# A decoder trunk on one core: another order at the ends of the feed forwards

## The chip, the cores and the metric

The kernel runs on one core of one Trainium2 chip. The metric is the device time of one execution in microseconds (us). The core's engines each work through their own list of instructions in order: PE multiplies matrices (PEld is its loading of weights), DVE and ACT work on tiles elementwise, POOL does a few additions, SP issues most of the transfers. An instruction waits until what it reads is written and what it overwrites has been read.

## The reference

Two layers, each a feed forward, a mixer and a second feed forward, on 512 tokens of 1024 channels in float32:

```
for l in range(2):
    x = x + 0.5 * swiglu(rms_norm(x, ffn1_norm[l]), gate1[l], up1[l], down1[l])
    u = rms_norm(x, mix_norm[l])
    ...                       # four branches on u (attention, convolution, sparse attention, retention)
    x = x + merged @ w_out[l]
    x = x + 0.5 * swiglu(rms_norm(x, ffn2_norm[l]), gate2[l], up2[l], down2[l])
swiglu(x) = (silu(x @ w_gate) * (x @ w_up)) @ w_down          # 1024 -> 2816 -> 1024
rms_norm(x, g) = x / sqrt(mean(x * x) + 1e-6) * g
```

## The kernel before, in words

Activations lie transposed: `XT[:, d]` holds channels 128 d to 128 d + 127 of all 512 tokens. Every float32 product is made as three products of rounded halves, hi x hi, hi x lo and lo x hi. So each weight block is split: ACT writes `whi` (L213), DVE subtracts and writes `wlo` (L214). Both lie in four rotating buffers, so the split of unit n waits until unit n - 4 has been multiplied.

A feed forward (`ffn`) goes through 11 pairs p of hidden tiles. The gate and up products of a pair are made by a seven-product scheme of Strassen's kind over 2 x 2 blocks: `comb_in` forms seven combinations of the input, the factors 0 to 6 (`Ahi`, `Alo` for 0 to 3, the tiles `E` for 4 to 6), for four groups c of two channel tiles each; DVE forms seven combinations of the weights (sums at L414). A product (`product`, L408) is 24 matmuls of 128 x 256, six for each group c. In program order a pair makes products 0 (bank `sc`), 1 (`pv`), 2 (`sc`), 3 (`tp`), 4 (`sc`), 5 (`tp`), 6 (`sc`). Between them ACT copies partial results out of the bank (`snap`, L389), and the next product that adds into the bank waits for that copy. At the end of a pair comes `h`, hi (L488, ACT) and lo (L489, DVE), which the down products read. They run in units between later pairs (`down_unit`, L525, matmuls of 128 x 512), and the last four pairs' (hidden tiles 14 to 21) in a tail of eight units, one for each output tile d. Each adds into `XT` on DVE (L527) and calls `done(d)`.

`done` starts what comes next on that tile: at the end of a first feed forward the mixer's norm (`norm_in`: hi, lo, a square on ACT, its sum into `acc` on POOL, L321), at the end of the first layer's second feed forward the same with `comb_in`, at the very end `flush(d)`: four transposes on PE (L1176), a copy on ACT (L1178), a store of 256 KB issued on ACT's queue (L1180). The w_out products in front of a second feed forward (L1161, add at L1162) call `norm_in` with `comb_in` too. `norm_end` sums `acc` over channels on PE (L327), takes the inverse root on DVE in twelve small rows, spreads it as a diagonal `z` (L335), multiplies it by ones (L339, ACT copies it out as `R`, L341). Its two results lie in bank `tp` (two buffers). The next feed forward calls it after its second product; only the end of the first pair (L482, L484) needs `R`.

`Line.go` prepares the weights of the unit three ahead of the one it runs, and the last units of one stretch prepare the first three of the next. A scheduler decides on each engine's list from this program order, priorities and its own estimate of times; a tile's buffers are given out in program order. `tc.issue_after(x)` holds all instructions traced in its block that are on x's engine behind x in that engine's list.

FFN1(l) and FFN2(l) are the feed forwards of layer l. FFN1(0) gets its factors from the input, FFN2(0) and FFN2(1) from w_out, FFN1(1) from the tail of FFN2(0).

Of the kernel before, what the change touches and what calls it, by code (L numbers as in the profile page):

```python
# [71 lines left out]
def body(tc, ins, out):  # L72
# [203 lines left out]
    def comb_in(d, gain, src=None):  # L276
# [10 lines left out]
        with tc.high_priority() if len(st["order"]) == 4 else ExitStack():  # L287
# [3 lines left out]
            dve.tensor_tensor(F[:, 4], F[:, 5], F[:, 7], op=OP.subtract)  # L291
            dve.scalar_tensor_tensor(F[:, 2], F[:, 4], -1.0, F[:, 0], op0=OP.mult, op1=OP.subtract)
            dve.tensor_tensor(lo[:, 0:2], F[:, 0:2], fv(hi[:, 0:2]), op=OP.subtract)  # L293
            dve.tensor_tensor(F[:, 3], F[:, 0], F[:, 7], op=OP.subtract)
            act.activation(hi[:, 2:4], F[:, 2:4], AF.Copy)
            dve.scalar_tensor_tensor(F[:, 6], F[:, 2], -1.0, F[:, 1], op0=OP.mult, op1=OP.subtract)
            dve.tensor_tensor(lo[:, 2:4], F[:, 2:4], fv(hi[:, 2:4]), op=OP.subtract)
            for u in range(3):
                act.activation(e[u][:, 0, c], F[:, 4 + u], AF.Copy)
                dve.tensor_tensor(e[u][:, 1, c], F[:, 4 + u], fv(e[u][:, 0, c]), op=OP.subtract)  # L300
# [11 lines left out]
    def norm_in(d, gain, comb=False):  # L312
        XT = ph["XT"]
        (comb_in if comb else split_in)(d, gain)
        if not ph["sq"]:
            ph["sq"] = True
            act.activation(st["acc"], XT[:, d], AF.Square)
        else:
            sq = ph["fp"].tile([128, T], F32, name="z", tag="z", bufs=2)
            act.activation(sq, XT[:, d], AF.Square)  # L320
            pool.tensor_tensor(st["acc"], st["acc"], sq, op=OP.add)  # L321

    def norm_end(ss=None):
        if ss is None:
            ss = tp_t()[:, :NT]
# [10 lines left out]
        ps = tp_t()  # L336
# [10 lines left out]
    class Line:  # L347
# [13 lines left out]
        def go(self, nxt=None):  # L361
            n = len(self.items)
            for i in range(n):
                self.prep(i + 1 + AHEAD)
# [5 lines left out]
    def ffn(wg, wu, wd, norm, done):  # L370
# [139 lines left out]
        def down_unit(f0, nf, d0, nd, l0, ln, end):  # L510

            def prep():
# [3 lines left out]
                return split(rawds[key][:, :, (d0 - l0) * 128:(d0 - l0 + nd) * 128], (nf, nd * 128), False)  # L516

            def run(w):
                whi, wlo = w
                for j in range(nd):  # L520
                    ps = mm_t()
                    for k in range(nf):
                        h, b = hs[(f0 + k) // 2], (f0 + k) % 2
                        for n, (x, s) in enumerate(((whi, 0), (whi, 1), (wlo, 0))):
                            pe.matmul(ps, x[:, k, j * 128:(j + 1) * 128], h[:, s, b], start=k == 0 and n == 0, stop=k == nf - 1 and n == 2)  # L525
                    XT = ph["XT"]
                    dve.scalar_tensor_tensor(XT[:, d0 + j], ps, 0.5, XT[:, d0 + j], op0=OP.mult, op1=OP.add)  # L527
                    if end:
                        done(d0 + j)

            return prep, run


# [719 lines left out]
```

## Time and profile before

| what | value |
|---|---|
| three runs | 2836.33, 2837.72, 2836.96 us, median 2836.96 |
| the profiled execution, its own time | 2836.33 us |
| its span, first to last instruction | 2834.6 us |
| busy: PE, DVE, ACT, POOL | 2782.0, 1941.5, 1266.1, 54.0 us |
[...]

The profile is of one execution. A PE row's time includes the pipeline's end, so rows overlap their successors: rates are read from start to start, idle time from the brackets behind a row.

### The profile page before, as it was taken

Reading aid. Unit: us, or ns where it says so; the run is one execution under the profiler, and the core shown is the slowest. Engines: PE = TensorE matmul, PEld = TensorE weight load, DVE = VectorE, ACT = ScalarE, POOL = GpSimd, SP = SyncE. Lnnn points to the kernel's source line nnn. Section 1 sums busy time; section 2 is a strip of 40 time slices with the busy share of each in tenths; the row PEclk is TensorE's granted clock in tenths of the full one; section 3 lists DMA queues with packets and bytes.
Section 4 is the critical chain, followed back from the end, with each engine's and each line's share of the span. In section 5 each row is a group of like instructions: output and inputs, shape, how many; then the busy total and the mean of one; then the engine's idle time right before and its main releaser. Section 6 shows DMA issues by size and latency. Waiting matters only on the chain.

```text
span 2834.6 us, 40078 instructions
## 1 busy us (share of the span) xinstructions
PE 2782.0 (98%) x16295; PEld 2352.9 (83%) x16295; DVE 1941.5 (68%) x3329; ACT 1266.1 (45%) x2012; POOL 54.0 (2%) x39
## 2 busy tenths in 40 slices
PE   6999999999999999999999999999999999999998
PEld 6999978788776688999889998777887657799996
DVE  7787755547567478786887866564565765888782
ACT  6444443433356355444544444343323663554441
POOL 0000010000000010000000001000000000100000
PEclk8999999999999999999999999999999999999999
DMA  4323332132420252323323233312324203423312
GB/s 140 115 86 109 117 101 89 42 121 60 149 90 1 66 172 75 111 91 97 120 75 118 83 97 116 103 60 75 117 71 137 60 1 89 159 95 101 112 57 74
DMA packets 238461, 265.94 MB, mean 94 GB/s; under 512 B 7292, under 2 KB 210884, under 8 KB 238276
## 3 DMA queue, kind: packets, MB, share of 16 engines
q1 hardware_dynamic: 233876, 261.20, 28.7%
q8 instruction: 128, 2.10, 0.3%
q10 hardware_dynamic: 4400, 2.17, 0.3%
q14 instruction: 57, 0.47, 0.1%
HBM read 257.06 MB, written 6.29 MB: 93 GB/s over the span
## 4 chain that ended last, share of the span: by engine, by line
PE 82%; DVE 2%; ACT 2%; issue 0%; DMA 0%; POOL 0%; ACTq 0%; DVEq 0%; POOLq 0%
PE mm L231 20%; PE sc L408 13%; PE mm L525 13%; PE mm L701 6%; PE tp L408 6%; PE mm L637 5%; PE mm L1161 3%; PE pv L969 3%; PE pv L408 3%; PE tp L959 2%; PE pv L637 2%; PE sc L921 1%; PE sc L922 1%; ACT whi L213 1%; PE tp L909 0%; DVE wlo L214 0%
## 5 line engine op out<-in xcount | busy, mean ns | idle before, releaser
L213 ACT ACTIVATE whi<-raw 128x1024 fp32r<-128x1024 f32 (+2 forms) x368 | 352.3, 958 | 757.0 <-PE mm L231 282.1
L214 DVE TENSOR_TENSOR wlo<-raw,whi 128x1024 fp32r<-128x1024 f32 (+2 forms) x368 | 402.8, 1098 | 185.1 <-ACT whi L213 178.8
L525 PE MATMUL mm<-h,whi 128*128 128x512 f32 x1408 | 445.4, 397 | 3.4 <-ACT h L488 2.7
L231 PE MATMUL mm<-Ahi,whi 128*128 128x512 f32 x864 | 342.2, 396 | 0.0
L231 PE MATMUL mm<-Ahi,wlo 128*128 128x512 f32 x864 | 340.6, 394 | 0.0
L231 PE MATMUL mm<-Alo,whi 128*128 128x512 f32 x864 | 340.3, 394 | 0.0
L525 PEld LDWEIGHTS mm<-h,whi 128*128 128x128 f32 x1408 | 260.9, 188 | 64.5 <-ACT h L488 3.5
L213 ACT ACTIVATE whi<-s 128x1024 fp32r<-128x1024 f32 x176 | 186.5, 1060 | 260.6 <-PE sc L408 71.7
L525 PE MATMUL mm<-h,wlo 128*128 128x512 f32 x704 | 278.8, 396 | 0.0
L214 DVE TENSOR_TENSOR wlo<-s,whi 128x1024 fp32r<-128x1024 f32 x176 | 214.6, 1219 | 46.1 <-ACT whi L213 45.5
L408 PE MATMUL sc<-E,whi 128*128 128x256 f32 x1408 | 225.1, 282 | 9.0 <-ACT sn L389 7.4
L408 PEld LDWEIGHTS sc<-E,whi 128*128 128x128 f32 x1408 | 192.0, 190 | 10.6 <-ACT sn L389 8.8
L527 DVE SCALAR_TENSOR_TENSOR XT<-mm,XT 128x512 f32<-128x512 f32 x128 | 88.0, 688 | 155.4 <-PE mm L525 155.4
L231 PEld LDWEIGHTS mm<-Ahi,wlo 128*128 128x128 f32 x864 | 162.5, 188 | 34.8 <-issue 3.6
L231 PEld LDWEIGHTS mm<-Ahi,whi 128*128 128x128 f32 x864 | 162.4, 188 | 34.9 <-issue 2.0
L231 PEld LDWEIGHTS mm<-Alo,whi 128*128 128x128 f32 x864 | 162.7, 188 | 31.6 <-issue 1.6
L213 ACT ACTIVATE whi<-rawd 128x1024 fp32r<-128x1024 f32 (+1 forms) x96 | 94.7, 989 | 150.5 <-PE sc L408 69.8
L525 PEld LDWEIGHTS mm<-h,wlo 128*128 128x128 f32 x704 | 132.6, 188 | 32.1
L408 PE MATMUL sc<-Ahi,whi 128*128 128x256 f32 x704 | 144.2, 287 | 6.0 <-ACT whi L213 3.8
L408 PE MATMUL sc<-Alo,whi 128*128 128x256 f32 x704 | 143.1, 285 | 2.5 <-DVE Alo L293 2.5
L214 DVE TENSOR_TENSOR wlo<-rawd,whi 128x1024 fp32r<-128x1024 f32 (+1 forms) x96 | 110.3, 1149 | 50.6 <-ACT whi L213 50.3
L408 PE MATMUL sc<-Ahi,wlo 128*128 128x256 f32 x704 | 142.7, 284 | 0.5 <-DVE wlo L214 0.5
(299 smaller groups left out, 5617.1 us busy)
## 6 DMA issues: line engine op xcount, KB each, us to landing
raw<-in_w_in_dram SPq DMA_DIRECT2D x66, 1024.0 KB, 6.8
raw<-in_ffn_w_gate_dram SPq DMA_DIRECT2D x44, 1024.0 KB, 5.3
raw<-in_ffn_w_up_dram SPq DMA_DIRECT2D x44, 1024.0 KB, 7.8
rawd<-in_ffn_w_down_dram SPq DMA_DIRECT2D x32, 1024.0 KB, 5.1
rawd<-in_ffn_w_down_dram SPq DMA_DIRECT2D x16, 768.0 KB, 4.4
raw<-in_w_branch_dram SPq DMA_DIRECT2D x8, 1024.0 KB, 7.6
raw<-in_w_branch_dram SPq DMA_DIRECT2D x16, 512.0 KB, 8.9
raw<-in_w_out_dram SPq DMA_DIRECT2D x8, 1024.0 KB, 8.6
```

Source lines behind the costliest of these rows:

```text
L213: act.activation(hi, src, AF.Copy)
L214: dve.tensor_tensor(lo, src, fv(hi), op=OP.subtract)
L231: pe.matmul(ps, x, y, start=first and j == 0, stop=last and j == len(passes) - 1)
L408: pe.matmul(ps[:, g * 256:(g + 1) * 256], x[:, g * 4 + c], factor(u, s, c), start=first and n == 0, stop=last and n >= 22, skip_group_chec ...
L525: pe.matmul(ps, x[:, k, j * 128:(j + 1) * 128], h[:, s, b], start=k == 0 and n == 0, stop=k == nf - 1 and n == 2)
L527: dve.scalar_tensor_tensor(XT[:, d0 + j], ps, 0.5, XT[:, d0 + j], op0=OP.mult, op1=OP.add)
L637: pe.matmul(ps[i][:, :n], a, w, start=kk == 0 and j == 0, stop=kk == KT - 1 and j == 2)
L701: pe.matmul(ps, x[:, k], v[:, k], start=k == 0 and j == 0, stop=k == 3 and j == 2)
L921: pe.matmul(ps[:, :n], q, kT[0][:, g, s0:s0 + n], start=True, stop=False)
L959: pe.transpose(ps[:, r * 128:(r + 1) * 128], P[4 * g + r][:, j * 128:(j + 1) * 128], ident)
L969: pv_last[0] = pe.matmul(pv[g * 64:(g + 1) * 64], V(g, j), pts[g], start=first and j == 0, stop=last and j == nblk - 1)
L1161: pe.matmul(ps, x[:, k], v, start=k == 0 and j == 0, stop=k == KT - 1 and j == 2)
```

## The change

In `comb_in` two DVE rows change places, and `st["made"]` keeps the last factor row. The last of the seven additions into `acc` goes from POOL to DVE, in the `comb` case behind `made`. `norm_end` takes its two results' banks from `mm` (three buffers) where a feed forward calls it, still from `tp` at the end of a first feed forward. `Line.go` puts what the first four units of a feed forward prepare (units 3 to 6) behind `made` on DVE. In the tail the unit d = 0 multiplies only its first six of eight hidden tiles (pairs 7 to 9), then d = 1 does so, then the two tiles of the last pair 10 follow for d = 0 and for d = 1. `flush(d)` is called one unit later.

```
@@ -289,15 +289,15 @@
             hi, lo, e = st["hi"][:, c], st["lo"][:, c], st["e"]
             act.activation(hi[:, 0:2], F[:, 0:2], AF.Copy)
             dve.tensor_tensor(F[:, 4], F[:, 5], F[:, 7], op=OP.subtract)
+            dve.tensor_tensor(lo[:, 0:2], F[:, 0:2], fv(hi[:, 0:2]), op=OP.subtract)
             dve.scalar_tensor_tensor(F[:, 2], F[:, 4], -1.0, F[:, 0], op0=OP.mult, op1=OP.subtract)
-            dve.tensor_tensor(lo[:, 0:2], F[:, 0:2], fv(hi[:, 0:2]), op=OP.subtract)
             dve.tensor_tensor(F[:, 3], F[:, 0], F[:, 7], op=OP.subtract)
             act.activation(hi[:, 2:4], F[:, 2:4], AF.Copy)
+            dve.tensor_tensor(lo[:, 2:4], F[:, 2:4], fv(hi[:, 2:4]), op=OP.subtract)
             dve.scalar_tensor_tensor(F[:, 6], F[:, 2], -1.0, F[:, 1], op0=OP.mult, op1=OP.subtract)
-            dve.tensor_tensor(lo[:, 2:4], F[:, 2:4], fv(hi[:, 2:4]), op=OP.subtract)
             for u in range(3):
                 act.activation(e[u][:, 0, c], F[:, 4 + u], AF.Copy)
-                dve.tensor_tensor(e[u][:, 1, c], F[:, 4 + u], fv(e[u][:, 0, c]), op=OP.subtract)
+                st["made"] = dve.tensor_tensor(e[u][:, 1, c], F[:, 4 + u], fv(e[u][:, 0, c]), op=OP.subtract)
 
     def factor(u, s, c):
         if u < 4:
@@ -313,16 +313,20 @@
         XT = ph["XT"]
         (comb_in if comb else split_in)(d, gain)
         if not ph["sq"]:
-            ph["sq"] = True
+            ph["sq"], ph["nsq"] = True, 0
             act.activation(st["acc"], XT[:, d], AF.Square)
         else:
             sq = ph["fp"].tile([128, T], F32, name="z", tag="z", bufs=2)
             act.activation(sq, XT[:, d], AF.Square)
-            pool.tensor_tensor(st["acc"], st["acc"], sq, op=OP.add)
-
-    def norm_end(ss=None):
+            ph["nsq"] += 1
+
+            with tc.issue_after(st["made"].ins) if comb and ph["nsq"] == 7 else ExitStack():
+                (dve if ph["nsq"] == 7 else pool).tensor_tensor(st["acc"], st["acc"], sq, op=OP.add)
+
+    def norm_end(ss=None, bank=None):
+        bank = bank or mm_t
         if ss is None:
-            ss = tp_t()[:, :NT]
+            ss = bank()[:, :NT]
             for i in range(NT):
                 pe.matmul(ss[:, i:i + 1], st["acc"][:, i * 128:(i + 1) * 128], ones[:, 0:1], start=True, stop=True)
         v = small([128, NT], name="nv", bufs=1)
@@ -333,7 +337,7 @@
         dg = ph["fp"].tile([128, T], F32, name="z", tag="z", bufs=2)
         for i in range(NT):
             dve.tensor_scalar(dg[:, i * 128:(i + 1) * 128], ident, rc[:, i:i + 1], None, op0=OP.mult)
-        ps = tp_t()
+        ps = bank()
         for i in range(NT):
             s = slice(i * 128, (i + 1) * 128)
             pe.matmul(ps[:, s], ones, dg[:, s], start=True, stop=True)
@@ -358,10 +362,11 @@
                 self.got.append(self.items[self.ready][0]())
                 self.ready += 1
 
-        def go(self, nxt=None):
+        def go(self, nxt=None, behind=None):
             n = len(self.items)
             for i in range(n):
-                self.prep(i + 1 + AHEAD)
+                with tc.issue_after(behind) if behind is not None and i < 4 else ExitStack():
+                    self.prep(i + 1 + AHEAD)
                 if nxt and i + 1 + AHEAD > n:
                     nxt.prep(i + 1 + AHEAD - n)
                 self.items[i][1](self.got[i])
@@ -507,46 +512,72 @@
             sp.dma_start(raw, wd[f0 * 128:(f0 + nf) * 128, d0 * 128:(d0 + nd) * 128].rearrange("(k p) n -> p k n", p=128))
             return raw
 
-        def down_unit(f0, nf, d0, nd, l0, ln, end):
+        def down_mm(ps, w, j, f0, k0, k1, nf):
+            whi, wlo = w
+            for k in range(k0, k1):
+                h, b = hs[(f0 + k) // 2], (f0 + k) % 2
+                for n, (x, s) in enumerate(((whi, 0), (whi, 1), (wlo, 0))):
+                    pe.matmul(ps, x[:, k, j * 128:(j + 1) * 128], h[:, s, b], start=k == 0 and n == 0, stop=k == nf - 1 and n == 2)
+
+        def down_add(d, ps):
+            XT = ph["XT"]
+            dve.scalar_tensor_tensor(XT[:, d], ps, 0.5, XT[:, d], op0=OP.mult, op1=OP.add)
+
+        def down_prep(f0, nf, d0, nd, l0, ln):
 
             def prep():
                 key = (f0, l0)
                 if key not in rawds:
                     rawds[key] = down_load(f0, nf, l0, ln)
                 return split(rawds[key][:, :, (d0 - l0) * 128:(d0 - l0 + nd) * 128], (nf, nd * 128), False)
-
+            return prep
+
+        def down_unit(f0, nf, d0, nd, l0, ln):
             def run(w):
-                whi, wlo = w
                 for j in range(nd):
                     ps = mm_t()
-                    for k in range(nf):
-                        h, b = hs[(f0 + k) // 2], (f0 + k) % 2
-                        for n, (x, s) in enumerate(((whi, 0), (whi, 1), (wlo, 0))):
-                            pe.matmul(ps, x[:, k, j * 128:(j + 1) * 128], h[:, s, b], start=k == 0 and n == 0, stop=k == nf - 1 and n == 2)
-                    XT = ph["XT"]
-                    dve.scalar_tensor_tensor(XT[:, d0 + j], ps, 0.5, XT[:, d0 + j], op0=OP.mult, op1=OP.add)
-                    if end:
-                        done(d0 + j)
-
-            return prep, run
+                    down_mm(ps, w, j, f0, 0, nf, nf)
+                    down_add(d0 + j, ps)
+            return down_prep(f0, nf, d0, nd, l0, ln), run
+
+        def last_unit(d):
+
+            def run(w):
+                ps = mm_t()
+                if d == 0:
+                    down_mm(ps, w, 0, 14, 0, 6, 8)
+                    rawds["kept"] = ps, w
+                    return
+                if d == 1:
+                    down_mm(ps, w, 0, 14, 0, 6, 8)
+                    p0, w0 = rawds.pop("kept")
+                    down_mm(p0, w0, 0, 14, 6, 8, 8)
+                    down_add(0, p0)
+                    done(0)
+                    down_mm(ps, w, 0, 14, 6, 8, 8)
+                else:
+                    down_mm(ps, w, 0, 14, 0, 8, 8)
+                down_add(d, ps)
+                done(d)
+            return down_prep(14, 8, d, 1, d // 2 * 2, 2), run
 
 
         down_at = {}
         for p0 in (0, 2):
             for k in range(2):
-                down_at[p0 + 2 + k] = tuple([down_unit(2 * p0, 4, 4 * k + 2 * q, 2, 4 * k, 4, False)] for q in range(2))
+                down_at[p0 + 2 + k] = tuple([down_unit(2 * p0, 4, 4 * k + 2 * q, 2, 4 * k, 4)] for q in range(2))
         for k in range(2):
-            down_at[7 + k] = tuple([down_unit(8, 6, 4 * k + 2 * q + j, 1, 4 * k + 2 * q, 2, False) for j in range(2)] for q in range(2))
+            down_at[7 + k] = tuple([down_unit(8, 6, 4 * k + 2 * q + j, 1, 4 * k + 2 * q, 2) for j in range(2)] for q in range(2))
         for p in range(NP):
             step(p)
         for d in range(KT):
-            tail.add(*down_unit(14, 8, d, 1, d // 2 * 2, 2, True))
+            tail.add(*last_unit(d))
         return main, tail
 
     def ffn_run(F, nxt=None):
         ph["two"] = True
         main, tail = F
-        main.go(tail)
+        main.go(tail, st["made"].ins)
         tail.go(nxt[0] if nxt else None)
 
 
@@ -1192,7 +1223,10 @@
     def to_next(l):
         def done(d):
             if l == L - 1:
-                flush(d)
+                if d:
+                    flush(d - 1)
+                if d == KT - 1:
+                    flush(d)
                 return
             if d == 0:
                 new_norm(True)
@@ -1211,7 +1245,7 @@
     for l in range(L):
         ffn_run(F)
         ph["two"] = False
-        norm_end()
+        norm_end(None, tp_t)
         leave("hp")
         leave("fp")
         F = ffn(*weights(2, l), norm_end, to_next(l))
```

In the rows below `sc`, `pv`, `tp`, `mm` are banks, numbers tell buffers apart, `y0` holds the combinations of one group c, `s` sums of weights, `raw` weights as loaded. Lines of the changed kernel have other numbers: L292, L293, L296 and L297 are L293, L292, L297 and L296 there, L408 is L413, L414 is L419, L327 and L339 are L331 and L343.

DVE at the start of FFN2(0), from the last w_out addition on, before:

```order
L1162 SCALAR_TENSOR_TENSOR XT_9112<-mm_9441,XT_9112 128x512
L214 TENSOR_TENSOR wlo_9490<-s_9433,whi_9489 128x1024
L291 TENSOR_TENSOR y0_9428<-y0_9428 128x256
L414 TENSOR_TENSOR s_9594<-s_9435,raw_9344 128x1024
L292 SCALAR_TENSOR_TENSOR y0_9428<-y0_9428 128x256
L293 TENSOR_TENSOR Alo_9122<-y0_9428,Ahi_9121 128x512
L296 SCALAR_TENSOR_TENSOR y0_9428<-y0_9428 128x256
L297 TENSOR_TENSOR Alo_9122<-y0_9428,Ahi_9121 128x512
L300 TENSOR_TENSOR E_9124<-y0_9428,E_9124 128x256
L300 TENSOR_TENSOR E_9125<-y0_9428,E_9125 128x256
L300 TENSOR_TENSOR E_9126<-y0_9428,E_9126 128x256
L214 TENSOR_TENSOR wlo_9523<-s_9520,whi_9522 128x1024
```

and of the change:

```order
L1193 SCALAR_TENSOR_TENSOR XT_9112<-mm_9441,XT_9112 128x512
L291 TENSOR_TENSOR y0_9428<-y0_9428 128x256
L293 SCALAR_TENSOR_TENSOR y0_9428<-y0_9428 128x256
L297 SCALAR_TENSOR_TENSOR y0_9428<-y0_9428 128x256
L292 TENSOR_TENSOR Alo_9122<-y0_9428,Ahi_9121 128x512
L296 TENSOR_TENSOR Alo_9122<-y0_9428,Ahi_9121 128x512
L300 TENSOR_TENSOR E_9124<-y0_9428,E_9124 128x256
L300 TENSOR_TENSOR E_9125<-y0_9428,E_9125 128x256
L300 TENSOR_TENSOR E_9126<-y0_9428,E_9126 128x256
L324 TENSOR_TENSOR acc_9123<-acc_9123,z_9482 128x512
L214 TENSOR_TENSOR wlo_9490<-s_9433,whi_9489 128x1024
L419 TENSOR_TENSOR s_9520<-raw_9344 128x1024
```

The two weight rows that stood among the factors of the last group stand behind them and behind the new addition. FFN1(1) and FFN2(1) show the same rows at their starts.

PE at the start of FFN2(0), where product 3 (`tp_9630`) begins, before (the 24 rows of product 4 in `sc_9493` end ahead of it):

```order
L408 MATMUL sc_9493<-E_9124,wlo_9523 128x256 x2
L408 MATMUL pv_9795<-Ahi_9121,whi_9689 128x256 x2
L339 MATMUL tp_9587<-z_9582,ones_66 128x128 x4
L408 MATMUL tp_9630<-Ahi_9121,whi_9489 128x256 x2
L408 MATMUL tp_9630<-Alo_9122,whi_9489 128x256 x2
```

and of the change, from the end of product 2 on, and below it the second piece of the norm:

```order
L413 MATMUL sc_9493<-Ahi_9121,whi_9437 128x256 x2
L413 MATMUL sc_9493<-Alo_9122,whi_9437 128x256 x2
L413 MATMUL sc_9493<-Ahi_9121,wlo_9438 128x256 x2
L413 MATMUL tp_9630<-Ahi_9121,whi_9489 128x256 x2
L413 MATMUL tp_9630<-Alo_9122,whi_9489 128x256 x2
```

```order
L413 MATMUL pv_9795<-Alo_9122,whi_9689 128x256 x2
L413 MATMUL pv_9795<-Ahi_9121,wlo_9690 128x256
L343 MATMUL mm_9587<-z_9582,ones_66 128x128 x4
L413 MATMUL pv_9795<-Ahi_9121,wlo_9690 128x256
L413 MATMUL pv_9795<-Ahi_9121,whi_9689 128x256 x2
```

Product 3, which had to wait for the norm's two turns in the `tp` buffers, stands between products 2 and 4, and the norm's second piece has moved from behind product 4 of the first pair into product 1 of the second pair (`pv_9795`). All four feed forwards have this order now.

PE in the last tail, from the last rows of the first six hidden tiles of d = 0 on, before (`h_24843` is pair 9, `h_25068` pair 10):

```order
L525 MATMUL mm_25075<-h_24843,wlo_24976 128x512
L525 MATMUL mm_25075<-h_25068,whi_24975 128x512 x2
L525 MATMUL mm_25075<-h_25068,wlo_24976 128x512
L525 MATMUL mm_25075<-h_25068,whi_24975 128x512 x2
L525 MATMUL mm_25075<-h_25068,wlo_24976 128x512
L1176 MATMUL mm_25101<-ident_64,XT_21687 128x128 x4
L525 MATMUL mm_25115<-h_24290,whi_25004 128x512 x2
L525 MATMUL mm_25115<-h_24290,wlo_25005 128x512
```

and of the change, from the last row of the first six hidden tiles of d = 1 on:

```order
L520 MATMUL mm_25100<-h_24843,wlo_25005 128x512
L520 MATMUL mm_25075<-h_25068,whi_24975 128x512 x2
L520 MATMUL mm_25075<-h_25068,wlo_24976 128x512
L520 MATMUL mm_25075<-h_25068,whi_24975 128x512 x2
L520 MATMUL mm_25075<-h_25068,wlo_24976 128x512
L520 MATMUL mm_25100<-h_25068,whi_25004 128x512 x2
L520 MATMUL mm_25100<-h_25068,wlo_25005 128x512
L520 MATMUL mm_25100<-h_25068,whi_25004 128x512 x2
L520 MATMUL mm_25100<-h_25068,wlo_25005 128x512
L1207 MATMUL mm_25133<-ident_64,XT_21687 128x128 x4
L520 MATMUL mm_25145<-h_24290,whi_25035 128x512 x2
```

Pair 10 is read after 36 matmuls of the tail, not 18, and the transposes of d = 0 stand behind the last matmul of d = 1. The list then goes on with 24 matmuls of the next d and the transposes of the one before it; the transposes of d = 6 and d = 7 stand at its end. SP's list is the same as before.

## Rows read from the trace of the kernel before

**Rows 1.** The page: busy time of each engine, share of the span and instructions

```profile
PE 2782.0 (98%) x16295; PEld 2352.9 (83%) x16295; DVE 1941.5 (68%) x3329; ACT 1266.1 (45%) x2012; POOL 54.0 (2%) x39
```

**Rows 2.** Waits of PE: us in total, times, longest

```profile
PE sc L408 <- ACT sn L389: 9.5, 9, 1.9
PE mm L1176 <- DVE XT L527: 6.3, 8, 0.8
PE tp L327 <- POOL acc L321: 1.5, 2, 0.7
```

**Rows 3.** Busy time in stretches: us, PE, PEld, DVE, ACT, POOL, clock, DMA

```profile
29.40:70.36 40.96, 33.21 (x250) 31.58 (x249) 35.09 (x53) 23.16 (x36) 0.00 (x0) 0.96 0.17 55
1067.87:1108.77 40.90, 36.28 (x282) 35.05 (x280) 31.63 (x50) 21.53 (x29) 1.46 (x1) 0.96 0.16 52
1420.58:1461.70 41.12, 36.90 (x281) 35.15 (x280) 30.63 (x49) 19.19 (x27) 1.45 (x1) 0.96 0.16 52
2462.36:2501.76 39.40, 34.80 (x281) 33.57 (x280) 31.53 (x50) 21.54 (x29) 1.45 (x1) 1.00 0.17 54
1108.77:1125.97 17.20, 17.20 (x145) 17.20 (x145) 17.10 (x18) 9.71 (x12) 0.00 (x0) 1.00 0.38 123
2768.03:2834.60 66.57, 53.44 (x226) 40.34 (x224) 17.41 (x18) 13.51 (x17) 0.00 (x0) 0.95 0.22 68
```

**Rows 4.** The chain that ended last, two pieces without a wait: start, us, rows

```profile
1114.74 5.69 PE sc L408 x48
1126.13 5.60 PE mm L525 x24
```

**Rows 5.** PE at the start of FFN2(0): start, us, row, idle before and releaser

```profile
1074.89 0.95 PE L327 MATMUL tp<-ones,acc 128*128 128x1 f32 x8
1076.88 0.53 PE L408 MATMUL sc<-Ahi,whi 128*128 128x256 f32 x2 [1.05 <-ACT sn L389]
...
1082.90 0.74 PE L408 MATMUL sc<-E,whi 128*128 128x256 f32 x4 [1.40 <-ACT sn L389]
...
1087.29 1.06 PE L339 MATMUL tp<-z,ones 128*128 128x128 f32 x8
```

**Rows 6.** ACT in the same stretch

```profile
1074.36 1.99 ACT L213 ACTIVATE whi<-s 128x1024 fp32r<-128x1024 f32 x2
```

**Rows 7.** DVE in the same stretch and at the first down unit behind it

```profile
1070.41 2.32 DVE L414 TENSOR_TENSOR s<-s,raw 128x1024 f32<-128x1024 f32 x1
...
1124.14 0.69 DVE L455 TENSOR_TENSOR O<-pv,sn 128x512 f32<-128x512 f32 x1
1124.74 1.22 DVE L214 TENSOR_TENSOR wlo<-s,whi 128x1024 fp32r<-128x1024 f32 x1
1125.87 1.22 DVE L489 TENSOR_TENSOR h<-O,h 128x1024 fp32r<-128x1024 f32 x1
```

**Rows 8.** POOL in the same stretch

```profile
1070.19 1.46 POOL L321 TENSOR_TENSOR acc<-acc,z 128x512 f32<-128x512 f32 x1 [3.54 <-ACT z L320]
```

**Rows 9.** PE at the start of FFN1(0)

```profile
67.39 0.74 PE L408 MATMUL sc<-E,whi 128*128 128x256 f32 x4 [1.87 <-ACT sn L389]
```

**Rows 10.** PE in the last tail

```profile
2774.63 0.49 PE L525 MATMUL mm<-h,whi 128*128 128x512 f32 x1 [2.24 <-ACT h L488]
2775.89 0.50 PE L525 MATMUL mm<-h,whi 128*128 128x512 f32 x1 [0.77 <-DVE h L489]
...
2778.98 1.20 PE L525 MATMUL mm<-h,whi 128*128 128x512 f32 x2
...
2787.84 0.66 PE L1176 MATMUL mm<-ident,XT 128*128 128x128 f32 x4 [0.78 <-DVE XT L527]
2788.25 0.71 PE L525 MATMUL mm<-h,whi 128*128 128x512 f32 x2
...
2830.09 0.66 PE L1176 MATMUL mm<-ident,XT 128*128 128x128 f32 x4 [0.78 <-DVE XT L527]
```

**Rows 11.** The stores of the output (L1180), from issue to landing

```profile
DMA to landing us min/median/max: 2.3/2.3/5.5
```

## Prediction

> **What bounds the kernel now.** PE's own work does: the page has it busy for 2782.0 of the span's 2834.6 us [rows 1]. So only time that PE loses can be won, and the reader should look for where it loses it. The waits of PE name the releasers that the change touches [rows 2]: 9.5 us for ACT's copies of partial sums (`sn`), 6.3 us for DVE's last addition ahead of the output's transposes, 1.5 us for POOL's sum of squares. A busy row can hide loss too: it counts the same at half the clock, and a row that starts late because its bank changes is still busy. So I do not add up idle time but compare, stretch by stretch, the length [rows 3] with the bare work. The chain of waits gives the rate when nothing waits: 48 matmuls of 128 x 256 in 5.69 us, 0.1185 each, and 24 of 128 x 512 in 5.60 us, 0.233 each [rows 4].
>
> Four stretches are the starts of the feed forwards, from the first products to product 4 of the second pair (to product 5 of it in FFN1(0)). FFN2(0) takes 40.90 us. Its bare work is 264 matmuls at 0.1185, 31.3, and the two pieces of the norm, 0.95 and about 0.85 (1.06 as shown less the overlapping end) [rows 5], in all 33.1 us. It loses 7.8. FFN1(1) loses 8.0 and FFN2(1) 6.3 by the same count [rows 3]. FFN1(0) has 240 matmuls and one piece of the norm from 29.40 to 70.36, 29.3 us bare, and loses 11.6. The fifth stretch is the last tail: from 2768.03 to the last transposes at 2830.09 are 62.1 us [rows 10], of which 8 x 5.60 = 44.8 are matmuls.
>
> Why the starts lose: DVE makes two weight rows in the middle of the last factors; one of them takes 2.32 us [rows 7] while POOL adds beside it [rows 8], and PE waits for `Alo`. Then ACT splits two units of weights, 1.99 us [rows 6], ahead of the copy that product 2 waits for; PE stands 1.05 us, and later 1.40 us for the next copy, with product 3 held back behind the norm, although its operands lie ready [rows 5].
>
> **The change part by part.** *Starts.* I walked through the two lists with the durations of the rows: 1.13 us for a DVE row of 1024, 0.60 for one of 512 [rows 7] and half of that for 256 (estimate), about 1.0 for an ACT split [rows 6]. In FFN2(0) the last factors need no weight row any more: the four `Alo` halves are there 4 us after the stretch begins, when PE comes to them after 29 matmuls, and the last of the squares' sum 5.6 us after it, when PE has done its 48. The copy of product 0 now stands ahead of the splits, so product 2 starts at some 6.7 us instead of 9.0. While ACT copies product 2, PE does product 3, 2.9 us, which covers the 1.40 us wait. Products 4, 5 and 6 and product 0 of the next pair then follow without a wait: their weights come 1 to 2 us ahead of need. The first new wait is at the norm's second piece: DVE reaches the end of `z` after eight weight rows, five sums, seven rows of 512, six of 256 and the norm's small rows, 23 us of work and 2 us of waits for ACT, at 25.5 us, and PE, five matmuls into product 1 of the second pair, is there at 24.6. I leave 1.0 us for it and 0.5 for changes of bank. Won: 7.8 - 1.5 = 6.3 in FFN2(0), 6.5 in FFN1(1), 4.8 in FFN2(1).
>
> In FFN1(0) the weights of product 2 are as late as before, 0.95 us in two waits that the change does not touch; product 3 then covers what PE waits for now in front of product 4, and the norm's piece has moved out of the way of everything up to the wait of 1.87 us for a copy at the end of the stretch [rows 9]. I leave another 0.5 for a copy behind a split, 0.6 for `z` and 0.5 for changes of bank: 11.6 - 2.6 = 9.0 won. But DVE has nothing to spare behind it: `h` of pair 1 comes about 0.9 us after the first down unit wants it. So 8.1. The four starts together give 25.7 us.
>
> Bounds for a start: nothing is won if all that DVE and ACT put off comes back as new waits, and no more than the whole loss can be won, 33.7 in the four.
>
> *The sum of squares on DVE.* At the end of a first feed forward PE waits 0.7 us for POOL, twice [rows 2]. The DVE row is 0.6 long where POOL's took over 1.2, DVE is idle there, and PE does one more matmul first: 1.4 in all, between 0 and 1.5.
>
> *The banks* themselves cost nothing: the three `mm` buffers are free where no down unit has begun, and what they do for the order is counted above.
>
> *The last tail.* Pair 10 is wanted after 36 matmuls, 8.4 us after 2768.03, at 2776.4. Its hi was there at 2774.6 and its lo at 2775.9 [rows 10], so the waits of 2.24 and 0.77 go, with over half a us to spare. The transposes of one tile (0.41 us, from 2787.84 to 2788.25) stand behind the next tile's 24 matmuls, so seven of the eight waits of 0.78 go; a tile now takes 7.04 us ((2830.09 - 2787.84) / 6), and will take 6.01. The matmuls at half the clock behind the first waits (the row at 2778.98 lasts 1.20 for two) have no wait ahead of them any more. New length: 44.8 + 7 x 0.41 + 0.94 for the last addition, 48.6 against 62.1, 13.5 won. The two last copies now come within 0.9 us of each other and ACT issues a store in between, which I take at 0.7. Won: 12.8. A store lands 2.3 us after its issue [rows 11]; of the two last ones I take it that they overlap without holding each other up for long. [...]
>
> Bounds for the tail: 5.5 if only the seven waits go and the rest comes back, 13.5.
>
> [...]
>
> Sum: 25.7 + 1.4 + 12.8 - 1.6 = 38.3. The profiled execution took 2836.33 us, so 2798.0; it lies 0.6 below the median of the runs, so **2799**.
>
> **The rivals.** *DVE becomes the bound of the starts.* From the last w_out addition to the lo half of pair 1's `h` the changed list has 50.1 us of DVE work (17 splits, 9 sums and the rest at the durations above; 48.4 before, since a sum has come in front and the new addition). PE will want that half 53.3 us after the addition. DVE can then afford 3 us of waits for ACT and PE in all, and by my walk has about that. Already now it is busy for 17.10 of 17.20 us ahead of that down unit [rows 3]. If each start has 3 us of such waits more, 12 to 13 of the 25.7 go: 2811. [...]
>
> *The starts give nothing*, since every wait removed returns at `z` or at `h`: 1.4 + 12.8 = 14.2 won, 2823. Against it: the operands of product 3 lie ready during the waits of now.
>
> *Slower.* `issue_after` holds the weights of four units behind the last factor. If they come late for each of the four units, and PE waits at each, the tail's gain can be eaten: to be slower by 0.2% the starts would have to lose 14.2 + 5.7 = 19.9 us, 5 each, some 1.25 at each of the units, a little over one DVE row. For it: one row more or less decides at `z`. Against it: DVE idles 9.3 of the 40.90 us now [rows 3], which a list without holes gives back.
>
> *No effect* would need the scheduler to keep its list; the rows of the change show that it did not.
>
> **How the numbers follow.** The forecast, 2791 to 2805 with the clock and the leftover waits either way: 0.62. DVE as the bound, 2805 to 2818: 0.23. Starts that give little, 2818 to 2831: 0.07. Slower: 0.03. Within 0.2% (5.7 us, about what a measurement of this kernel can tell from no change): 0.02. Below 2791: 0.03. The range runs from 2791 to 2815 and leaves out under 2 in 10. Faster 0.95, the same 0.02, slower 0.03.
>
> **What would show it.** In the profile after: no wait of 2.24 us at `h` and only one wait of PE ahead of transposes; PE waits for `sn` down from 9.5 to 3 us or less; the four stretches at 32 to 35 us; a wait of about 1 us at the norm's second piece in the second pair (right) or of 3 us and more there or at a down unit's `h` (the DVE rival); no wait for `acc` on POOL. I am wrong if the tail has a new wait for weights of the later tiles, or if the starts' waits move to `wlo`.

## The result and the profile after

The changed kernel takes 2791.45 us (median of four runs, 2790.99 to 2791.60), the kernel before 2836.68 beside it (2836.33 to 2837.72): a ratio of 0.984, interval 0.9823 to 0.9857. The forecast was 2799 in 2791 to 2815, so the result lies only 0.45 us above the lower end of the range. The profiled execution took 2791.41 us with a span of 2789.6, so 44.9 us less than the one shown of before.

The page's busy line of the changed kernel, to be held against [rows 1]:

```profile
PE 2766.9 (99%) x16295; PEld 2345.1 (84%) x16295; DVE 1940.2 (70%) x3334; ACT 1264.4 (45%) x2012; POOL 45.6 (2%) x34
```

What PE waits for, changed kernel (us in total, times, longest), against [rows 2]:

```profile
PE tp L133 <- DMA z<-in_ffn_norm_dram: 6.4, 1, 6.4
PE mm L143 <- ACT XT L145: 4.5, 3, 2.4
PE sc L413 <- ACT whi L213: 3.3, 2, 3.1
...
PE sc L413 <- DVE wlo L214: 0.5, 1, 0.5
...
PE mm L1207 <- DVE XT L524: 0.4, 1, 0.4
PE tp L343 <- DVE z L339: 0.4, 2, 0.2
PE tp L413 <- ACT sn L394: 0.3, 1, 0.3
```

`sn` falls from 9.5 to 0.3 us, the output's transposes (L1207) from eight waits to one, and POOL's `acc` is gone. The first three rows, 14.2 us, belong to the beginning of the program, which the change does not touch.

The starts and the last tail in windows of the changed kernel (columns as in [rows 3]). Each start has the first 264 matmuls of the products; in the three later ones and in the tail that is the same work as in [rows 3], in FFN1(0) the window there begins later and holds 240 matmuls and a piece of the norm:

```profile
21.90:57.12 35.22, 34.14 (x265) 33.31 (x265) 35.02 (x56) 24.96 (x45) 0.00 (x0) 0.95 0.27 90
1058.62:1092.42 33.80, 33.70 (x281) 33.29 (x280) 31.71 (x52) 20.85 (x28) 0.00 (x0) 1.00 0.20 63
1403.37:1437.12 33.75, 33.70 (x282) 33.26 (x280) 31.67 (x52) 19.57 (x27) 0.00 (x0) 1.00 0.20 63
2436.78:2470.59 33.81, 33.71 (x282) 33.30 (x280) 31.71 (x52) 20.84 (x28) 0.00 (x0) 1.00 0.20 63
2736.75:2789.63 52.88, 48.59 (x226) 39.07 (x224) 17.41 (x18) 13.30 (x17) 0.00 (x0) 1.00 0.28 87
```

The three later starts, 40.90, 41.12 and 39.40 us before, now take 33.8 alike, 0.7 above the bare work of 33.1, at a granted clock of 1.00. The last tail took 66.5 and takes 52.9.

To place all of the gain, and for the experiments, I took five lengths from each trace: in each feed forward from the start of its first product to that of its first down unit (for FFN2(0) before, 40.90 + 17.20 in [rows 3]), and the last tail from its first matmul to the end of the span.

| kernel | FFN1(0) | FFN2(0) | FFN1(1) | FFN2(1) | last tail | median, us |
|---|---|---|---|---|---|---|
| before | 63.21 | 58.10 | 58.30 | 56.58 | 66.52 | 2836.68 |
| changed | 53.49 | 50.88 | 50.83 | 50.89 | 52.88 | 2791.45 |
| order on DVE, norm in `tp` (e1) | 64.54 | 57.24 | 58.20 | 57.25 | 52.89 | 2821.10 |
| before, norm in `mm` (e8) | 53.96 | 52.69 | 51.98 | 52.74 | 66.51 | 2812.52 |
| norm called later, in `tp` (e10) | 55.98 | 50.84 | 50.85 | 50.86 | 52.88 | 2793.99 |
| weights not held behind (e2) | 53.66 | 52.28 | 50.85 | 52.25 | 52.89 | 2795.04 |
| last addition on POOL (e3) | 53.45 | 51.52 | 51.57 | 51.54 | 52.89 | 2796.31 |
| factor rows back (e4) | 54.14 | 50.89 | 50.86 | 50.89 | 52.89 | 2792.42 |
| two DVE rows more (e12) | 53.64 | 50.89 | 50.86 | 50.89 | 52.89 | 2791.48 |
| six DVE rows more (e13) | 53.88 | 52.28 | 52.26 | 52.28 | 52.89 | 2796.70 |
| tail undone (e5) | 53.71 | 50.89 | 50.86 | 50.89 | 66.53 | 2806.20 |
| transposes early (e6) | 53.40 | 50.90 | 50.86 | 50.88 | 59.36 | 2798.29 |
| pair early (e7) | 54.08 | 50.90 | 50.86 | 50.89 | 52.96 | 2792.97 |
| less on ACT (e14) | 55.45 | 50.89 | 50.86 | 50.89 | 52.89 | 2794.01 |

The gain is 30.1 us in the starts (9.7, 7.2, 7.5, 5.7) and 13.6 in the tail. At the ends of the first feed forwards and of FFN2(0) it is another 1.8 (0.15, 0.91, 0.75), and the beginning lost 0.5 (first product at 21.90 instead of 21.35): 45.0. The last two figures are not clear of scatter: the stretches around the ends of the first feed forwards differ by up to 0.9 among kernels that leave them alone, and the first product starts between 20.90 and 22.12 in kernels that leave the beginning alone. The medians of before beside the runs e1, e2, e5, e8 / e3, e6, e7, e10 / e4, e12 to e14 were 2837.4, 2838.5 and 2838.7, single runs 2832.5 to 2841.1. The kernels with the change repeat within 1.5 us, and their lengths, where nothing was edited, within some 0.05 us except in FFN1(0), where they scatter by 0.7. For the lengths of before there is the one trace alone, with a stretch at half the clock in three of its four starts (a granted clock of 0.50 from 1428.9 to 1432.1 us, for one; [rows 3]: 0.96, 0.96, 0.96 and 1.00).

### The profile page after: what moved, and what is told of

Read it like the earlier page. It is cut to its first block, busy times and chain, and to the rows that moved or that the text cites. A ratio compares the mean times of both kernels' runs of the same rounds, so it can differ in the third digit from the quotient of the medians.

```text
span 2789.6 us, 40049 instructions
## 1 busy us (share of the span) xinstructions
PE 2766.9 (99%) x16295; PEld 2345.1 (84%) x16295; DVE 1940.2 (70%) x3334; ACT 1264.4 (45%) x2012; POOL 45.6 (2%) x34
## 4 chain that ended last, share of the span: by engine, by line
PE 97%; ACT 1%; DVE 1%; issue 0%; DMA 0%; ACTq 0%
PE mm L231 20%; PE sc L413 18%; PE mm L520 18%; PE tp L413 9%; PE mm L732 6%; PE mm L668 5%; PE pv L413 4%; PE mm L1192 3%; PE pv L1000 3%; PE tp L990 2%; PE pv L668 2%; PE sc L952 1%; PE sc L953 1%; PE tp L940 1%; PE sc L1047 0%; ACT whi L213 0%
## 5 line engine op out<-in xcount | busy, mean ns | idle before, releaser
L413 PE MATMUL sc<-E,whi 128*128 128x256 f32 x1408 | 224.2, 281 | 0.0
L413 PEld LDWEIGHTS sc<-E,whi 128*128 128x128 f32 x1408 | 192.1, 190 | 0.0
L413 PE MATMUL sc<-Ahi,whi 128*128 128x256 f32 x704 | 142.0, 283 | 3.3 <-ACT whi L213 3.3
L413 PE MATMUL sc<-Ahi,wlo 128*128 128x256 f32 x704 | 141.4, 282 | 0.5 <-DVE wlo L214 0.5
L413 PE MATMUL sc<-Alo,whi 128*128 128x256 f32 x704 | 141.5, 282 | 0.0
L413 PE MATMUL sc<-E,wlo 128*128 128x256 f32 x704 | 141.2, 282 | 0.1
```

The lines of the kernel that those rows point to most:

```text
L413: pe.matmul(ps[:, g * 256:(g + 1) * 256], x[:, g * 4 + c], factor(u, s, c), start=first and n == 0, stop=last and n >= 22, skip_group_chec ...
```

## Experiments

**What makes the gain of the starts: the order on DVE, or product 3?** e1 puts only the norm back:

```
-        bank = bank or mm_t
+        bank = bank or tp_t
```

> The changed kernel with both results of the norm back in the banks tp, all else kept. Product 3 then stands again behind the norm's second piece, products 2 and 4 one behind the other. If product 3 in between is what covers ACT's copies (my theory), each start gets back a wait of PE of 1.4 us (1.9 in the first) for the copy in front of product 4 and some of the next one, 6 to 11 us in four starts: 2797 to 2803. If the order on DVE alone makes the gain of the starts (rival), 2791 to 2793.

Measured: 2821.1. All of the gain of the starts is gone, more than my theory had. The 1.0 us by which the four starts are longer than before (64.54, 57.24, 58.20, 57.25) is no more than one fall of the clock costs (1.6 by an estimate: 0.04 x 41 us in a start at 0.96, [rows 3]): in FFN2(1) this kernel has one (a granted clock of 0.80 from 2474 to 2480 us) and the trace of before has none. PE at the start of FFN2(0) of this kernel, then the window behind these rows, and last a row of the kernel before at the same product:

```profile
1078.83 0.74 PE L413 MATMUL sc<-E,whi 128*128 128x256 f32 x4 [0.69 <-ACT sn L394]
...
1082.86 0.50 PE L413 MATMUL pv<-Ahi,whi 128*128 128x256 f32 x2 [0.91 <-ACT whi L213]
...
1084.66 0.58 PE L413 MATMUL pv<-Ahi,wlo 128*128 128x256 f32 x2 [1.06 <-DVE wlo L214]
1085.04 0.63 PE L413 MATMUL pv<-Ahi,whi 128*128 128x256 f32 x2
```

```profile
1082.00:1088.00 6.00, 4.08 (x20) 3.88 (x21) 5.83 (x15) 0.81 (x1) 0.00 (x0) 0.74 0.99 320
```

```profile
1086.95 0.51 PE L408 MATMUL pv<-Ahi,whi 128*128 128x256 f32 x2 [0.91 <-ACT whi L213]
```

The copy is less late than before (0.69 for 1.40 in [rows 5]), but with product 3 held behind the norm PE runs on into the second pair's product 1 (`pv`). The wait of 0.91 for its `whi` was there before too; before, the norm's second piece and product 3 then came, and now PE goes on and waits 1.06 for `wlo`. The next copy, which cost 0.43 before (at 1108.77), costs 0.93 here (at 1108.24), and in part of the stretch the granted clock falls (0.74 over the 6 us of the window; from 1085.04 on pairs of matmuls begin 0.43 apart, before it 0.24). What DVE's list saves in front returns behind. That the late `wlo` comes from DVE's new order is my reading; no run takes it apart.

e8 is the other half alone, the kernel before with this edit:

```
-    def norm_end(ss=None):
+    def norm_end(ss=None, bank=None):
+        bank = bank or mm_t
...
-            ss = tp_t()[:, :NT]
+            ss = bank()[:, :NT]
...
-        ps = tp_t()
+        ps = bank()
...
-        norm_end()
+        norm_end(None, tp_t)
```

> The kernel before with one edit: the norm's results lie in the banks mm where a feed forward calls it. If both edits are needed (my theory), FFN1(0), whose list of DVE has no such weight rows, gains its whole 9 to 10 us, the other three 2 to 4 each of their 5.7 to 7.5: 2815 to 2822. If the order on DVE makes the gain (rival), 2833 to 2837; if the banks alone make it (the other rival), 2806 to 2808, all 30 of the starts.

Measured: 2812.5, between the two theories: 24.8 of the 30.1 us come from this edit alone (9.3, 5.4, 6.3, 3.8). Some 4.9 of them are the clock (an estimate: 0.04 x 41 us in each of the three starts at 0.96 in [rows 3]; here it is 1.00 from 1057 to 1110 and from 1400 to 1460 us, and 0.94 from 20 to 70, with the beginning of the program in it). Its waits of PE, and for comparison one of the kernel before:

```profile
PE sc L409 <- DVE Alo L293: 2.5, 3, 0.8
...
PE sc L409 <- ACT sn L390: 0.9, 2, 0.5
```

```profile
PE sc L408 <- DVE Alo L293: 2.5, 3, 0.8
```

The late factors cost 0.8 in each of three starts, just as before; what goes is the wait for copies, `sn` from 9.5 to 0.9.

e10 asks whether it is the bank, or the place that the bank gave to product 3:

```
-        bank = bank or mm_t
+        bank = bank or tp_t
...
                 dve.tensor_tensor(v["O"][:, :, 0, 0], half(py), half(v["sn1"]), op=OP.add)
-                if p == 0:
-                    norm()
...
                 v["Z"] = snap(v["z"], "sn3")
+                if p == 0:
+                    norm()
```

> The changed kernel with the norm's results back in the banks tp, but the norm called behind product 3 and its copy instead of behind product 2. If only the place of product 3 matters (my theory by now), the starts keep their gain in another bank too: 2790 to 2794. If the norm must have banks of its own, since in tp its second piece now waits for product 5 and the next pair's product 3 behind it (rival), 2 to 5 us are lost in each start: 2800 to 2812.

Measured: 2794.0, as the theory has it. In three starts the lengths are those of the changed kernel to 0.04 us: the bank does not matter, the place does. Only FFN1(0) is 2.5 longer: there the second pair's products 2 and 4 stand one behind the other again, with the norm's second piece and product 3 behind them, and PE shows the old wait for a copy that stands behind a split, which itself had waited for PE (PE, then ACT):

```profile
55.26 0.74 PE L413 MATMUL sc<-E,whi 128*128 128x256 f32 x4 [1.46 <-ACT sn L394]
...
59.04 1.16 PE L343 MATMUL tp<-z,ones 128*128 128x128 f32 x8 [0.66 <-DVE z L339]
```

```profile
53.66 1.06 ACT L213 ACTIVATE whi<-raw 128x1024 fp32r<-128x1024 f32 x1 [1.00 <-PE sc L413]
54.62 0.58 ACT L394 ACTIVATE sn<-sc 128x512 f32<-128x512 f32 x1
```

**The rest of the starts.** e2, e3 and e4 each take back one part of DVE's order:

```
e2-        main.go(tail, st["made"].ins)
e2+        main.go(tail)
...
e3-            with tc.issue_after(st["made"].ins) if comb and ph["nsq"] == 7 else ExitStack():
e3-                (dve if ph["nsq"] == 7 else pool).tensor_tensor(st["acc"], st["acc"], sq, op=OP.add)
e3+            pool.tensor_tensor(st["acc"], st["acc"], sq, op=OP.add)
```

and e4 exchanges the two pairs of rows in `comb_in` back, as the first hunk of the diff reads upwards.

> The changed kernel without the rule that puts the weights of the first four units behind the last factor. Two weight rows of DVE stand among the factors of the last group again, in three of the four starts. If the late factors cost PE its time (my theory), 1 to 2.5 us are lost in each of the three, and nothing in FFN1(0): 2794.5 to 2799. If the banks alone make the gain of the starts (rival), since product 3 can now run while the factors are late, 2791 to 2793.

> The changed kernel with the last addition of the sum of squares on POOL as before. My term: at two ends of a first feed forward PE waits 0.7 us for it again, 1.4 in all, and at the starts POOL's addition lies beside DVE's rows, where a row of 1.2 us took 2.3 before, 0 to 1 each: 2793 to 2796. If POOL's addition is hidden once the other edits are there (rival): 2791 to 2792.

> The changed kernel with the two pairs of factor rows of DVE in their old order, lo behind the next combination. If this exchange costs and gives nothing by itself, since all of them stand ahead of the weights (my theory), 2791 to 2792.5. If the earlier lo is what PE waits for (rival), 0.4 to 0.8 in each of three starts: 2792.5 to 2794.

e2 loses 1.4 us in FFN2(0) and in FFN2(1), by another wait than I expected: not for a factor but for a copy. There the scheduler sets product 3 ahead of product 2, all but three of its matmuls, and then almost nothing stands between products 2 and 4:

```profile
1072.26 0.74 PE L413 MATMUL sc<-E,whi 128*128 128x256 f32 x4 [1.04 <-ACT sn L394]
```

In FFN1(1) product 3 stayed between them, and nothing is lost.

e3 loses 0.6 to 0.7 in each of the three starts and 2.2 around the two ends of the first feed forwards, the two waits of 0.73 for POOL among them; the rest there is within the scatter of these stretches. In a start a row of DVE is slow beside POOL's addition, and PE waits for the factor behind it (POOL, DVE and PE of e3):

```profile
1062.13 1.41 POOL L323 TENSOR_TENSOR acc<-acc,z 128x512 f32<-128x512 f32 x1 [3.21 <-ACT z L320]
```

```profile
1061.96 0.43 DVE L293 SCALAR_TENSOR_TENSOR y<-y 128x256 f32<-128x256 f32 x1
1062.42 1.41 DVE L297 SCALAR_TENSOR_TENSOR y<-y 128x256 f32<-128x256 f32 x1
```

```profile
1064.48 0.50 PE L412 MATMUL sc<-Alo,whi 128*128 128x256 f32 x2 [0.82 <-DVE Alo L292]
```

A row of 128 x 256 takes 0.43 when it begins ahead of POOL's row and 1.41 when it begins inside it; then it ends 0.29 behind POOL's end. The row of 2.32 in [rows 7] shows the same: it ends 1.08 behind the end of POOL's row in [rows 8]. What makes the later row wait is not taken apart by any run.

e4 moved nothing in the three later starts, because the scheduler undoes the exchange: in the last group of factors it puts both combinations ahead of both `lo` rows with and without it, as the list of the change ahead of the prediction shows for FFN2(0). DVE's and ACT's lists differ only in an earlier group of FFN2(0) and FFN2(1), PE's not at all. So the exchange is worth 0 in this kernel; what an earlier `lo` would give is not tested.

**How near DVE is to its bound.** e12 and e13 put two and six more rows of 0.60 us behind the sum of squares (e13 has a 6 for the 2):

```
+                for _ in range(2 if comb and ph["nsq"] == 7 else 0):
+                    dve.tensor_tensor(sq, sq, sq, op=OP.add)
```

> The changed kernel with two more rows of 128 x 512 on DVE behind the sum of squares (they double a tile that nothing reads any more), 1.2 us of work in each of three starts. If DVE has only some half a us to spare up to h of pair 1 (my reading of the trace after), each start loses 0.7: 2792.5 to 2794.5. If holes in DVE's list take them in (rival), 2791 to 2792.

> The same with six rows more, 3.6 us in each of three starts. If DVE is the next bound (my theory, the rival of the prediction just not reached), some 3 us are lost in each: 2799 to 2802, with waits of PE at weights, at the norm's second piece or at h of pair 1. If DVE is not near its bound, 2791 to 2794.

1.2 us more cost nothing, 3.6 cost 1.4 in each start. So in the changed kernel DVE has more than 1.2 us to spare, some 2.2 if the rest was taken in as well. Part of this is the scheduler's doing: PE's list is another one in both, with the norm's second piece 2.3 us (e12) and 2.5 us (e13) later in the stretch. The price is paid at weights, not at the norm or at `h`; what PE waits for in e13:

```profile
PE pv L415 <- ACT whi L213: 2.7, 3, 0.9
PE tp L415 <- ACT whi L213: 0.6, 3, 0.2
```

**The last tail.** e5 undoes both parts, e6 has the transposes early, e7 the last pair:

```
e5, e7-                if d == 0:
e5, e7+                if False:
...
e5, e7-                if d == 1:
e5, e7+                if False:
...
e5, e6-                if d:
e5, e6-                    flush(d - 1)
e5, e6-                if d == KT - 1:
e5, e6-                    flush(d)
e5, e6+                flush(d)
```

> The changed kernel with the last tails as before: eight tiles in turn, each output tile's transposes right behind its own addition. If the tail's term stands by itself (my theory), the 13.6 us that the trace shows there are lost, 2804 to 2806, with waits of 2.2 and 0.8 us at the last pair's h and seven of 0.8 ahead of transposes. If part of it hangs on what runs earlier, the last pair's h coming sooner now (rival), 2798 to 2802.

> The changed kernel with the transposes of each output tile right behind its addition again, the last inner pair still late. If the two parts of the last tail add up (my theory), eight waits of 0.78 come back, less the one of 0.44 that stays, and 0.25 at each new start: 7 to 8 us, 2798 to 2800. If such waits also bring the clock down (rival), 2801 to 2804.

> The changed kernel with the eight tiles of the last tail in turn, so that the last inner pair is wanted after 18 matmuls again, the transposes still one tile late. If the parts add up (my theory), the waits of 2.24 and 0.77 at h come back, in each of the four tails where h is late, but at the last one above all: 3 us, and 2 to 3.5 more for a stretch at half the clock behind them: 2796.5 to 2798. If the fall of the clock needs the wait ahead of the transposes as well (rival), 3 us alone: 2794 to 2795.

e5 gives back 13.65 us, with the old waits of 2.2 and 0.8 at `h` and eight of 0.8: the tail's term stands by itself. e6 gives back 6.5: seven waits, and a period of 7.04 where it is 6.03:

```profile
PE mm L1207 <- DVE XT L524: 5.5, 7, 0.8
```

e7 gives back 0.1 in the tail instead of 3 to 6.5, so both theories fell. With the transposes out of the way the scheduler itself sets eleven matmuls of d = 1 ahead of the last pair's first one for d = 0, and four more between that one and the next (counted from PE's waits for semaphores). So PE comes to the hi of that `h` at 2745.28, which ACT finished at 2745.08, and waits nowhere in the tail but once at its end:

```profile
2738.52:2791.48 52.96, 48.66 (x226) 39.00 (x224) 17.43 (x18) 13.32 (x17) 0.00 (x0) 1.00 0.29 87
```

So the later `flush` alone brings all of the 13.6 us; the code that splits the units 0 and 1 is worth 7.2 only where the transposes stay early (e5 against e6), and 0.1 here.

**What is left.** The longest waits now lie ahead of the first product. e14 takes work from ACT there:

```
+            if d % 2:
+                dve.tensor_copy(XT[:, d, :], ps)
+            else:
                 act.activation(XT[:, d, :], ps, AF.Copy)
...
+                if src is not None and u:
+                    pool.tensor_copy(e[u][:, 0, c], F[:, 4 + u])
+                else:
                     act.activation(e[u][:, 0, c], F[:, 4 + u], AF.Copy)
```

> A try at what is left: at the beginning of the program ACT works without a hole from 8.3 us on, and the first product starts at 21.9, when it has split the first weights. Here four of the eight copies of the input go to DVE and two of three hi copies of the factors E to POOL, 1.4 us of ACT's 5.0 for each group of channels. If ACT alone holds the first product up (theory), it starts 2 to 4 us sooner: 2787 to 2790. If DVE becomes the bound there, or POOL's rows slow DVE's (rival), 2791 to 2794.

The first product starts at 22.42, not sooner than in the other kernels (20.90 to 22.12), and FFN1(0) is 2 us longer. The input's transposes wait 6.6 us in all for copies out of their banks, 4.5 before this edit; which of the two rivals makes it, DVE's or POOL's rows, is not taken apart:

```profile
PE mm L143 <- ACT XT L148: 3.7, 2, 3.6
...
PE mm L143 <- DVE XT L146: 1.9, 1, 1.9
...
PE mm L143 <- ACT Ahi L293: 1.0, 1, 1.0
```

No kernel here beats the changed one.

## Why the prediction was right, and by how much its terms were off

*Direction and main cause held, the size just*: 44.9 us where 38.3 were forecast, with 0.45 us to the end of the range. Starts, tail and clock all came out better than forecast (by 4.4, 0.8 and 1.6), so the errors added up instead of cancelling, and that the result still lies in the range is in part luck. The promised signs came: no wait of 2.24 at `h`, one wait ahead of transposes, `sn` at 0.3, no `acc`, the three later stretches at 33.8. One did not: the wait of about 1 us at the norm's second piece.

*The starts, 25.7 forecast, 30.1 measured.* Two leftovers were mis-sized. First, 1.0 at `z` in each later start. DVE and PE of the changed kernel there, with DVE's `h` of pair 1 below:

```profile
1081.98 1.22 DVE L214 TENSOR_TENSOR wlo<-s,whi 128x1024 fp32r<-128x1024 f32 x1
1083.12 0.87 DVE L339 TENSOR_SCALAR z<-ident,rc 128x128 f32<-128x128 f32 x4
...
1109.46 1.21 DVE L494 TENSOR_TENSOR h<-O,h 128x1024 fp32r<-128x1024 f32 x1
```

```profile
1083.08 0.28 PE L413 MATMUL pv<-Ahi,wlo 128*128 128x256 f32 x1
1083.46 1.16 PE L343 MATMUL mm<-z,ones 128*128 128x128 f32 x8
1084.37 0.36 PE L413 MATMUL pv<-Ahi,wlo 128*128 128x256 f32 x1
```

Both engines come where my walk had them: DVE ends `z` 25.4 us after the stretch's start (25.5 forecast), and PE is there after 24.6 (24.6), one matmul of 0.12 behind the row at 1083.08. What was wrong is that PE waits for the end: `z` is four rows of a quarter each, PE's rows read quarter by quarter, and they begin 0.34 after DVE's first one. The wait costs about 0.3: PE begins 0.26 late, and the piece takes 0.91 up to the next matmul where I had 0.85. The 0.5 for changes of bank was about right in size, since 0.7 is left in all above the bare work, but not in place: of the 17 changes of bank in FFN2(0)'s start the rows at 1061.37 and 1061.70 begin 0.11 and 0.09 late, two changes lie at `z`, and the other 13 cost 0.01 at most; of the remaining rows that begin about 0.1 late (at 1062.65, 1065.77, 1078.82 and 1088.84) none changes its bank. Second, in FFN1(0) the 0.6 for `z` came as about 0.2, the 0.5 for a copy as 0.3 (the last of the waits above) and the 0.9 at `h` of pair 1 not at all: 9.7 for 8.1. "DVE has nothing to spare behind it" was the step that failed; for the three later starts e12 shows over 1.2 us to spare, and FFN1(0), of which that step spoke, shows no wait at `h` (that start was not loaded with more rows, so how much it has to spare stays open).

*Why the starts lose* was told too evenly. I put DVE's weight rows first and the held product 3 second. e8 and e1 show that the second makes 24.8 alone and the first nothing alone, 5.3 on top of it; e10 shows that it is the place of product 3, in whatever bank.

*The sum of squares on DVE, 1.4 forecast.* Right for the waits at the ends (two of 0.73 in e3; the stretches around them gained 1.1 from before to after, within their scatter), too small in all: e3 shows 0.6 to 0.7 more in each of three starts, which I had counted among the factors.

*The tail, 12.8 forecast, 13.6 measured.* The 0.7 for the two last copies did not come. PE's last rows and the store's line in the changed kernel:

```profile
2747.93 0.60 PE L1207 MATMUL mm<-ident,XT 128*128 128x128 f32 x4
...
2784.12 0.60 PE L1207 MATMUL mm<-ident,XT 128*128 128x128 f32 x4
2785.15 0.63 PE L1207 MATMUL mm<-ident,XT 128*128 128x128 f32 x4 [0.44 <-DVE XT L524]
```

```profile
DMA to landing us min/median/max: 2.3/2.3/2.6
```

A tile takes (2784.12 - 2747.93) / 6 = 6.03, as forecast, and from the last transposes to the end pass 4.5 us, as before (2830.09 in [rows 10] to the span's end): ACT's copies are 1.1 apart and do not meet. The last two stores, issued 1.1 apart at 2785.38 and 2786.49, landed after 2.3 each like one alone; the 2.6 is that of the first, issued at 2750.04. None of the eight held up another. But the split into two causes, waits at `h` to one edit and waits at transposes to the other, was wrong (e7).

*The clock, 1.6 lost forecast.* No run of the changed kernel shows this term, which was my estimate of one fall to half the clock in four starts (0.04 x 41 us, from the 0.96 in [rows 3]): the three later starts and the tail have 1.00, and the 0.95 of FFN1(0) lies at its very beginning (0.50 up to 25.6 us), behind the waits of the program's start.

*The rivals.* DVE as the bound is near but was not reached (e12, e13). A row held behind one that waits is seen on ACT in e10's FFN1(0), where the copy stands behind a split that waits 1.00 for PE. Starts that give nothing are what e1 is: the order without the place. The late weights of the rival on the other side are also seen there, 1.06 us that the kernel before did not have at this place in FFN2(0), but not in the changed kernel.

## What to carry to other kernels

Before making late operands earlier, look for work whose operands lie ready and ask what holds it back: here one product, held only by two turns of a bank, was worth 24.8 of 30.1 us, some 4.9 for the clock among them (the estimate of e8). Take edits apart in both directions: one alone can be worth nothing, as the order on DVE was, and one in place can make another superfluous, as the later `flush` did with the split of two units. Look at the lists before reading a run: an edit that the scheduler undoes, as in e4, tests nothing. And where a producer writes in pieces and the consumer reads in pieces, ask when the first piece is there: PE began 0.34 us after DVE's first row of `z`, whose four rows took 0.87.

## What the hardware showed that I had not expected

A small DVE row beside an addition on POOL took 1.41 us for 0.43. In these two rows what is added is about the rest of POOL's row, not a share of speed: 0.98 where POOL had 1.12 to go (e3), 1.10 for the bigger row of [rows 7], where it had 1.24 to go.

And PE's granted clock does not follow the length or the number of the waits in any simple way in these traces. It fell behind waits of 0.69, 0.91 and 1.06 us (0.74 over 6 us in e1). It stayed at 1.00 behind a single wait of 1.04 (e2), behind 1.46 and then 0.66 in FFN1(0) of e10, and through seven of 0.78, one every 7.04 us (e6). But in the kernel before it fell in FFN1(1) behind one of 0.80 at 1426.41 and the norm's first piece, and not in FFN2(1) behind 0.81, 1.05, 1.40 and 0.91:

```profile
1428.00:1438.00 10.00, 8.27 (x53) 7.78 (x52) 8.42 (x16) 3.50 (x6) 0.00 (x0) 0.83 0.15 41
2470.00:2480.00 10.00, 6.64 (x52) 6.16 (x52) 9.65 (x25) 3.92 (x5) 0.00 (x0) 1.00 0.21 63
```

So a forecast can carry such a fall only as a chance, as the 1.6 of this one was meant.
